# First layer's last modulation round moved out of the mixing into the output projection: products and sums on VectorE

## The chip, the core and the metric

The kernel runs on one core of one Trainium2 chip. The metric is the device time of one execution in microseconds (us), as the median of several runs. The engines are named as in the profile: PE (TensorE matmuls; PEld is its weight load), DVE (VectorE), ACT (ScalarE), POOL (GpSimd) and SP (SyncE, which here only issues DMAs). Each engine runs its own queue in order.

## The reference

The program is a diffusion backbone with two trunk layers, 512 latent tokens and 256 context tokens of width 1024, in fp32. Cut to what matters here, one layer is:

```python
def modulation(cvec, w_mod, b_mod):
    m = (jax.nn.silu(cvec) @ w_mod + b_mod)[..., None, :]
    return jnp.split(m, 6, axis=-1)

def trunk_layer(...):
    sh1, sc1, ga1, sh2, sc2, ga2 = modulation(c, w_mod, b_mod)
    sh1c, sc1c, ga1c, sh2c, sc2c, ga2c = modulation(c_ctx[None], w_mod, b_mod)
    u = (rmsnorm(x, g_mix) * (1 + sc1) + sh1) @ w_in
    ...
    mix = jnp.concatenate([pool_mixer(...), gla_output(...), latent_attention(...)], axis=-1) @ w_out
    x = x + ga1 * mix
    x = x + ga2 * squared_relu_mlp(rmsnorm(x, g_mlp) * (1 + sc2) + sh2, w_up, w_down)
    # in the first layer the context tokens get the same with their own six vectors
```

`w_mod` is 1024 x 6144 for each layer. Its six groups of 1024 columns give shift, scale and gate of the mixing (sh1, sc1, ga1) and of the MLP (sh2, sc2, ga2), for two streams: the latent tokens (from c) and the context tokens (from c_ctx). The MLP's scale sc2 is needed at the first norm before the MLP, and its gate ga2 only when the MLP's first results are added to X.

## The kernel before

All large products are fp32 split into a high and a low part, in three passes: hi x hi, hi x lo and lo x hi. A weight tile arrives by DMA as `raw` (three buffers), ACT makes its high part `whi` (L159) and DVE the low part `wlo` (L78). High and low parts live in two rings of buffers, tags "hi" and "lo", five each.

The modulation of a layer is made in three rounds of 2048 columns. Round 0 is (sh1, sc1), round 1 is (ga1, sh2), round 2 is (sc2, ga2). In the first layer rounds 1 and 2 are the function `modulation_round`. For each of eight k-steps it loads two 512 KB tiles `rawm` straight into buffers of the "hi" and "lo" rings, and PE multiplies them by the two streams' vectors, `sstat`, in four column groups of a PSUM tile `pm` (L190). `mod_end` then adds the bias row `brow` on DVE (L199), transposes on PE (L202), copies to `modT` on DVE (L203), and for gates writes rows to a DRAM tensor `gaD` with DMAs issued by POOL (L209). `load_ga` reads a gate back, spread over 128 partitions, with a DMA issued by ACT.

These rounds run inside the mixing stage, as a generator that is advanced one step at a time. A string for each layer, `STEPS`, gives the order: g is a step of the gated linear attention (GLA), a of the projections, m of the modulation and t of the softmax attention. In the first layer, `STEPS` has sixteen m, eight for each of the two rounds. The second layer's modulation is made elsewhere, during the first layer's MLP: `modulation_sums` forms the products and sums on DVE (L229, the first on ACT, L227), and PE only adds the 128 partitions of the sum up with a selecting matrix `osel` (L238).

After the mixing come, in order:

- the output projection. The first 512 columns of `w_out` are made for six token tiles, 24 matmuls each, in the PSUM tiles `op` (three buffers). The second 512 columns are made in three pairs of tiles (two buffers of a pair each). For each tile `out_res` multiplies by the gate into `rtmp` on DVE (L1162) and adds to the residual `X` (L1163; POOL for the first half of the columns, DVE for the second). A pair whose columns are complete is normalized by `norm_pair`: squares and sums on ACT (L275), the reciprocal root `rstd` on POOL, `xn` on DVE (L285), transposes `ptr` on PE (L292), then scale and shift by `scT` and `shT` into `h2h` (ACT, L300) and `h2l` (L305).
- the first up block of the MLP (`fm_pair`, L330), interleaved with the last pairs' transposes, and then the other blocks of up and down.

A scheduler puts the instructions of each engine in order when the program is built, from the order of the code and the buffers; on the chip that order is fixed.

Of the kernel before, what the change touches and what calls it, by code (L numbers as in the profile page):

```python
# [10 lines left out]
F32 = mybir.dt.float32  # L11
F32R = mybir.dt.float32r
I32 = mybir.dt.int32
AF = mybir.ActivationFunctionType
ALU = mybir.AluOpType
# [6 lines left out]
KT = 8  # L22
# [2 lines left out]
LEVELS = (1, 2, 4, 8, 16, 32, 64)  # L25
C_GV, C_GG, C_R, C_AQ = 768, 1024, 1280, 1312
GT = 5
STEPS = ("agamagamgaamgaagmaagmagamagamagamagagamagamagamagamgaamgaagmaagmagamagamttgtgttg"
         "tgttgtttgttgttttgttttgtt",
         "aaggggagaggaaagaaggaaaaaagaaaagaaaggaagaaggatatgatttttgaatgt"  # L30
         "tgtttgggtttgttggttttgtttgt")
# [3 lines left out]
def hybrid_kernel(ctx, tc, x, c, cx, c_ctx, w_mod, b_mod, g_mix, w_in, w_pool, s_pool, w_gate, b_gate,  # L35
                  g_gla, g_q, g_k, w_out, g_mlp, w_up, w_down, g_final, k_mask, k_rope, k_edge, k_invw, out):
    nc = tc.nc
    V, A, G, T = nc.vector, nc.scalar, nc.gpsimd, nc.tensor
# [3 lines left out]
    wp = ctx.enter_context(tc.tile_pool(name="wp", bufs=5))  # L42
# [9 lines left out]
    def nm(s):  # L52
        uid[0] += 1
        return f"{s}_{uid[0]}"

    def slot(s, dt=F32, w=NT):
        return sp.tile([128, w], dt, tag="S", name=nm(s))

    def wide(s, dt=F32):

        return sp.tile([128, 2 * NT + 32], dt, tag="W", name=nm(s), bufs=2)
# [12 lines left out]
    def psC(s):  # L74
        return pc.tile([128, 512], F32, tag="pc", name=nm(s))
# [11 lines left out]
    ident = const.tile([128, 128], F32, name="ident")  # L87
    make_identity(nc, ident)

    osel = const.tile([128, 2, 32], F32, name="osel")  # L90
# [21 lines left out]
    sstat = const.tile([128, KT, 32], F32, name="sstat")  # L112
# [31 lines left out]
    def wload(*srcs, sl=False):  # L144

        shp = [128, srcs[0].shape[1], sum(s_.shape[2] for s_ in srcs)]
        n = shp[1] * shp[2]
        raw = wp.tile([128, n], F32, tag="raw", name=nm("raw"), bufs=3)
        rv = raw.rearrange("p (a b) -> p a b", b=shp[2])
        o = 0  # L150
        for s_ in srcs:
            nc.sync.dma_start(rv[:, :, o:o + s_.shape[2]], s_)
            o += s_.shape[2]
        if sl:
            hi, lo = slot("whi", F32R, w=n), slot("wlo", F32R, w=n)
        else:
            hi = wp.tile([128, n], F32R, tag="hi", name=nm("whi"))
            lo = wp.tile([128, n], F32R, tag="lo", name=nm("wlo"))
        A.activation(hi, raw, AF.Copy)  # L159
        sub_lo(lo, raw, hi)  # L160
        return hi.rearrange("p (a b) -> p a b", b=shp[2]), lo.rearrange("p (a b) -> p a b", b=shp[2])

    def wcols(w, c0, n, ksplit, *more, sl=False):

        parts = []
        step = KT // ksplit
        for s in range(ksplit):
            parts.append(wload(*(w[s * step * 128:(s + 1) * step * 128, a:a + m].rearrange("(k p) n -> p k n", p=128)
                                 for a, m in ((c0, n),) + more), sl=sl))
        return lambda k: (parts[k // step][0][:, k % step], parts[k // step][1][:, k % step])  # L170
# [7 lines left out]
    gaD = dp.tile([2, 2, 2, D], F32, name="gaD")  # L178
    xD = dp.tile([NL, D], F32, name="xD")

    def modulation_round(l, r, modT):
        pm = psC("pm")
        for k in range(KT):
            yield
            for h in range(2):
                raw = wp.tile([128, 1024], F32, tag="lo" if h else "hi", name=nm("rawm"))
                c0 = r * 2048 + h * 1024
                nc.sync.dma_start(raw, w_mod[l, k * 128:(k + 1) * 128, c0:c0 + 1024])
                for j in (2 * h, 2 * h + 1):
                    T.matmul(pm[32 * j:32 * j + 32, :], sstat[:, k, :], raw[:, (j % 2) * 512:(j % 2) * 512 + 512],  # L190
                             start=(k == 0), stop=(k == KT - 1), skip_group_check=True)
        mod_end(l, r, modT, pm)
# [18 lines left out]
    def modulation_sums(l, r, modT, streams):  # L211
# [27 lines left out]
                             start=(s == 0), stop=(s == streams - 1), skip_group_check=True)  # L239
        mod_end(l, r, modT, pm)  # L240

    def mod_vec(modT, idx, s):

        r, j0 = idx // 2, (idx % 2) * 2
        return modT[:, r, j0:j0 + 2, :, s]

    def load_ga(l, which, s):
        t = bp.tile([128, D], F32, tag="ga", name=nm("ga"), bufs=2)
        nc.scalar.dma_start(t, gaD[l, which, s].partition_broadcast(128))
        return t  # L250
# [56 lines left out]
    def new_hT(s):  # L307
        return [(slot(s + "h", F32R), slot(s + "l", F32R)) for _ in range(KT)]
# [79 lines left out]
    def fin_scale(l, M, which):  # L388
        modT, scT, shT = M
        o = l * NV + 8 * which  # L390
        g_ = vec[:, o:o + 8].rearrange("p (j c) -> p j c", j=2)
        for s in range(2):
            V.scalar_tensor_tensor(scT[:, which, s].rearrange("p (j c) -> p j c", j=2), mod_vec(modT, 3 * which + 1, s),
                                   1.0, g_, ALU.add, ALU.mult)
            V.tensor_copy(shT[:, which, s].rearrange("p (j c) -> p j c", j=2), mod_vec(modT, 3 * which, s))

    def run(g):
        for _ in g:
            pass
# [9 lines left out]

    def mod_rest(l, M):  # L410
        yield from modulation_round(l, 1, M[0])
        yield from modulation_round(l, 2, M[0])
        fin_scale(l, M, 1)

    def mod_all(l, M):
        yield from modulation_sums(l, 0, M[0], 2)
# [6 lines left out]
    MODS = [None, None]  # L423
    for l in range(2):
        both = l == 0
# [6 lines left out]
        modT, scT, shT = MODS[l]  # L432
        hT = hT1 if l else new_hT("hT")
        if l == 0:
# [4 lines left out]
            rawm = {}  # L439
# [695 lines left out]
        ths = {"g": gla_thread(), "a": at_, "m": mods, "t": att_}  # L1135
        for ch in STEPS[l]:
            if ch == "t":
# [13 lines left out]
        for p2 in range(len(live) // 2):  # L1151
            XP[p2] = bp.tile([128, 2, D], F32, tag=f"X{p2}", name=nm("X"))
            t0 = 2 * p2 * 128
            src = xD[t0:t0 + 256] if l else (x[0, t0:t0 + 256] if p2 < 2 else cx[0])
            nc.scalar.dma_start(XP[p2], src.rearrange("(t p) d -> p t d", p=128))
            X[2 * p2], X[2 * p2 + 1] = XP[p2][:, 0], XP[p2][:, 1]
        ga = [load_ga(l, 0, s) for s in range(2 if both else 1)]
        def out_res(t, cb, ps):

            sl = slice(cb * 512, (cb + 1) * 512)  # L1160
            tmp = bp.tile([128, 512], F32, tag="rtmp", name=nm("rtmp"), bufs=2)
            V.tensor_tensor(tmp, ps, ga[0 if t < 4 else 1][:, sl], ALU.mult)  # L1162
            (V if cb else G).tensor_tensor(X[t][:, sl], X[t][:, sl], tmp, ALU.add)  # L1163

        np_ = len(live) // 2
        wk = wcols(w_out[l], 0, 512, 4)
        for t in live:
            ps = psB("op")
            tm_matmul(ps, t, wk, mixT, KT)
            out_res(t, 0, ps)  # L1170
        h2 = new_hT("h2")
        msc, msh = [scT[:, 1, s] for s in range(2)], [shT[:, 1, s] for s in range(2)]
        wk = wcols(w_out[l], 512, 512, 4)
        for p2 in range(np_):
            ps = psA("op")
            for i in range(2):
                tm_matmul(ps[:, i * 512:(i + 1) * 512], 2 * p2 + i, wk, mixT, KT)
                if p2 and i == 0:
                    norm_pair(p2 - 1, X, h2, msc, msh, psB)
                out_res(2 * p2 + i, 1, ps[:, i * 512:(i + 1) * 512])  # L1180


        ga = [load_ga(l, 1, s) for s in range(2 if both else 1)]
        NB = HID // 512
        pend = None

# [32 lines left out]
        for b in range(NB):  # L1219
            act = []  # L1220
            for i in range(4):
                nj = 2 if both else 4
                if b == 0 and i < nj:
                    if i == 0:
                        wks = [wcols(w_up[l], j * 128, 128, 1) for j in range(nj)]
                        pss = [psA("up") for j in range(2)]
                        if nj > 2:
                            pss = [p_[:, h * 512:h * 512 + 512] for p_ in pss for h in range(2)]
                        for p2 in range(np_):
                            if p2 == np_ - 1:  # L1230
                                norm_pair(p2, X, h2, msc, msh, psB)
                            for j in range(nj):
                                fm_pair(pss[j], wks[j], h2, KT, p2)
                    ps = pss[i]
                else:
                    wk = wcols(w_up[l], b * 512 + i * 128, 128, 1)
                    ps = psA("up")
                    fm_matmul(ps, wk, h2, KT, True, both)
                r_ = slot("relu")
                A.activation(r_[:, 0:N_], ps[:, 0:N_], AF.Relu)  # L1240
                if b % 2 and i < 2:
                    w_ = wide("a", F32R)
                    ah, al = w_[:, 0:NT], w_[:, NT:2 * NT]
                else:
                    ah, al = slot("ah", F32R), slot("al", F32R)
                V.tensor_tensor(r_[:, 0:N_], r_[:, 0:N_], r_[:, 0:N_], ALU.mult)
                A.activation(ah[:, 0:N_], r_[:, 0:N_], AF.Copy)
                sub_lo(al[:, 0:N_], r_[:, 0:N_], ah[:, 0:N_])
                act.append((ah, al))
                next(mods, None)  # L1250
            if pend is not None:
                down(*pend)
            pend = (act, b)
# [88 lines left out]
```

## Time and profile before

| what | value |
|---|---|
| median of 3 runs | 1676.79 us (1674.35 to 1676.84) |
| profiled execution: its own time | 1671.28 us |
| profiled execution: span | 1669.1 us |
| mean granted clock of TensorE | 0.985 |
| first matmul of the first layer's output projection | 363.86 us after the span's start |
| last wait in the first up block, before the matmuls of its third and fourth tile | until 460.5 us |

A row of the page's groups or of the timeline names line, engine, operation, output tile <- input tiles, and durations; "[x <-DVE rtmp]" says how long the engine was idle before and which instruction released it. The rows of the window view give, after the stretch and its length, the busy time and number of instructions of PE, PEld, DVE, ACT and POOL, then the granted clock, the DMA share and GB/s. Durations come from the one profiled execution, whose time is 0.3% below the median of the three runs.

### The profile page before, as it was taken

What the parts mean: (1) busy time and instruction counts of PE and PEld (TensorE: products, weight loads), DVE (VectorE), ACT (ScalarE), POOL (GpSimd) and SP (SyncE); (2) the same over time, 40 slices, a digit from 0 to 9 for tenths busy, and PEclk for the clock granted to TensorE, in tenths of its full rate; (3) what the DMA queues carried; (4) which work ended last, traced back from release to release, by engine and by line L of the source; (5) the groups of instructions that cost most, each with busy time, mean ns of one, the idle gap of its engine ahead of it and who ended that gap; (6) DMA issues with size and microseconds to landing.
All of it is one profiled execution on the core that took longest, in us unless ns stands there. A gap on an engine that the chain in (4) does not pass through costs nothing.

```text
span 1669.1 us, 27434 instructions
## 1 busy us (share of the span) xinstructions
PE 1595.7 (96%) x11403; PEld 1306.2 (78%) x11403; DVE 923.3 (55%) x1330; ACT 630.9 (38%) x1074; POOL 406.4 (24%) x476
## 2 busy tenths in 40 slices
PE   7999979999999999999999999897999999999997
PEld 4888856678888888888888789785667888888886
DVE  5437666753673654636546563587763545455554
ACT  5545445561531312213113234555662523223332
POOL 1121311212303041130321462241201122222224
PEclk9999989999999999999999999998999999999999
DMA  9445400222340422515424332100032313333331
GB/s 330 128 135 175 149 2 7 98 93 59 102 139 26 141 97 59 176 50 172 150 65 170 103 108 81 40 2 2 33 121 75 111 54 101 101 101 101 101 101 51
DMA packets 136636, 163.31 MB, mean 98 GB/s; under 512 B 9908, under 2 KB 108608, under 8 KB 136512
## 3 DMA queue, kind: packets, MB, share of 16 engines
q1 hardware_dynamic: 130176, 148.41, 27.9%
q10 hardware_dynamic: 5824, 13.12, 2.1%
q8 instruction: 89, 1.46, 0.4%
q14 instruction: 35, 0.29, 0.1%
q0 software_dynamic: 512, 0.03, 0.0%
HBM read 157.31 MB, written 4.23 MB: 97 GB/s over the span
## 4 chain that ended last, share of the span: by engine, by line
PE 84%; DVE 6%; ACT 4%; DMA 2%; issue 2%; POOL 2%; SPq 0%; ACTq 0%; DVEq 0%; POOLq 0%
PE dn L340 25%; PE up L321 19%; PE tm L340 7%; PE op L340 6%; PE up L323 5%; PE fm L321 4%; PE av L1071 3%; PE pT L1054 2%; PE up L330 2%; PE fm L323 1%; PE sc L1033 1%; PE att L769 1%; PE sc L1034 1%; DVE nmx L1036 1%; PE pm L190 1%
## 5 line engine op out<-in xcount | busy, mean ns | idle before, releaser
L159 ACT ACTIVATE whi<-raw 128x1024 fp32r<-128x1024 f32 (+2 forms) x182 | 185.3, 1033 | 568.0 <-PE dn L340 293.0
L1194 POOL TENSOR_TENSOR X<-X,rtmp 128x512 f32<-128x512 f32 x158 | 216.1, 1370 | 640.4 <-DVE rtmp L1193 640.1
L78 DVE TENSOR_TENSOR wlo<-raw,whi 128x1024 fp32r<-128x1024 f32 (+2 forms) x182 | 223.6, 1237 | 213.4 <-ACT whi L159 211.7
L1193 DVE TENSOR_TENSOR rtmp<-dn,ga 128x512 f32<-128x512 f32 x160 | 109.5, 689 | 212.8 <-PE dn L340 211.3
L340 PE MATMUL dn<-whi,ah 128*128 128x512 f32 x480 | 187.3, 390 | 0.6 <-ACT whi L159 0.6
L340 PE MATMUL dn<-whi,al 128*128 128x512 f32 x480 | 187.2, 390 | 0.0
L340 PE MATMUL dn<-wlo,ah 128*128 128x512 f32 x480 | 186.2, 390 | 0.0
L321 PE MATMUL up<-h2h,whi 128*128 128x512 f32 x464 | 182.5, 393 | 1.5 <-ACT relu L1240 1.5
L321 PE MATMUL up<-h2h,wlo 128*128 128x512 f32 x464 | 182.9, 394 | 0.0
L321 PE MATMUL up<-h2l,whi 128*128 128x512 f32 x464 | 182.4, 393 | 0.0
L340 PEld LDWEIGHTS dn<-whi,ah 128*128 128x128 f32 x480 | 90.1, 188 | 22.0 <-ACT whi L159 1.0
L321 PEld LDWEIGHTS up<-h2h,whi 128*128 128x128 f32 x464 | 87.1, 188 | 24.1 <-ACT relu L1240 1.7
L340 PEld LDWEIGHTS dn<-wlo,ah 128*128 128x128 f32 x480 | 90.1, 188 | 19.5 <-DVE wlo L78 0.5
L340 PEld LDWEIGHTS dn<-whi,al 128*128 128x128 f32 x480 | 90.1, 188 | 19.4
L340 PE MATMUL tm<-whi,hTh 128*128 128x256 f32 (+1 forms) x352 | 102.3, 292 | 1.1 <-ACT UV L891 1.1
L321 PEld LDWEIGHTS up<-h2h,wlo 128*128 128x128 f32 x464 | 87.1, 188 | 19.6
L321 PEld LDWEIGHTS up<-h2l,whi 128*128 128x128 f32 x464 | 87.1, 188 | 19.3
L340 PE MATMUL tm<-whi,hTl 128*128 128x256 f32 (+1 forms) x352 | 100.7, 287 | 0.0
L340 PE MATMUL dn<-whi,a 128*128 128x512 f32 x320 | 100.0, 395 | 0.4 <-DVE rtmp L1193 0.4
L340 PE MATMUL tm<-wlo,hTh 128*128 128x256 f32 (+1 forms) x352 | 100.2, 288 | 0.0
L229 DVE SCALAR_TENSOR_TENSOR macc<-rawm,sstat,macc 128x1024 f32<-128x1024 f32 x56 | 76.3, 1383 | 8.2 <-DMA rawm<-in_w_mod_dram 7.7
L1036 DVE TENSOR_REDUCE nmx<-sc 128x1 f32<-128x768 f32 x64 | 60.5, 955 | 24.1 <-PE sc L1034 23.3
(293 smaller groups left out, 3320.6 us busy)
## 6 DMA issues: line engine op xcount, KB each, us to landing
rawm<-in_w_mod_dram SPq DMA_DIRECT2D x80, 512.0 KB, 5.2
raw<-in_w_up_dram SPq DMA_DIRECT2D x64, 512.0 KB, 4.5
raw<-in_w_down_dram SPq DMA_DIRECT2D x64, 512.0 KB, 4.6
raw<-in_w_in_dram SPq DMA_DIRECT2D x26, 512.0 KB, 3.9
rawm<-in_w_mod_dram SPq DMA_DIRECT2D x32, 256.0 KB, 5.3
raw<-in_w_out_dram SPq DMA_DIRECT2D x16, 512.0 KB, 4.7
raw<-in_w_in_dram SPq DMA_DIRECT2D x12, 256.0 KB, 2.8
ga<-gaD ACTq DMA_DIRECT2D x6, 512.0 KB
```

The lines of the kernel that those rows point to most:

```text
L78: V.tensor_tensor(lo, full, hi.bitcast(F32), ALU.subtract)
L159: A.activation(hi, raw, AF.Copy)
L229: V.scalar_tensor_tensor(acc[s], raw, c_, acc[s], ALU.mult, ALU.add)
L321: T.matmul(ps[:, 0:NL], a, b[:, 0:NL], start=st, stop=sp_)
L323: T.matmul(ps[:, NL:NT], a, b[:, NL:NT], start=st, stop=sp_)
L330: T.matmul(ps[:, cs], a, b[:, cs], start=(k == 0 and i == 0), stop=(k == nk - 1 and i == 2))
L340: T.matmul(ps, a[:, sl], bb, start=(k == 0 and i == 0), stop=(k == nk - 1 and i == 2))
L1036: V.tensor_reduce(nmx[:, i:i + 1], sv, AX.X, ALU.max, negate=True)
L1054: T.transpose(pt_[:, i * 128:(i + 1) * 128], p_[:, ki * 128:(ki + 1) * 128], ident)
L1071: T.matmul(av_[64 * hh:64 * hh + 64, 0:256], vst, pe[:, hh * 256:hh * 256 + 256], start=(ki == 1), stop=(ki == len(kts) - 2))
L1193: V.tensor_tensor(tmp, ps, ga[0 if t < 4 else 1][:, sl], ALU.mult)
L1194: (V if b == NB - 1 and not both and t == 3 else G).tensor_tensor(X[t][:, sl], X[t][:, sl], tmp, ALU.add)
```

## The change

Round 2 of the first layer leaves the mixing. Eight of the sixteen m of `STEPS` are removed. A new generator `modulation_half` makes 1024 columns of a round: for each of eight k-steps one 512 KB load, and for each of the two streams a multiply-add into an accumulator `acc` (named macc) on DVE; for k = 0 two scaled copies on ACT. At the end eight matmuls of 256 columns with `osel` add up the partitions, then follow bias, two transposes and copies to `modT`. The first half is sc2, then comes `fin_scale`, which makes scT and shT; the second half is ga2, which ends with eight DMAs to `gaD` from POOL. The generator `mod_late` is advanced one step before the first projection tile and two steps after each tile; what is left runs before the MLP. The two gate loads of the first layer's MLP move behind the up matmuls of block 1, ahead of the first down block. The second layer is as before.

```diff
-STEPS = ("agamagamgaamgaagmaagmagamagamagamagagamagamagagamagamgaamgaagmaagmagamagamttgtgttg"
+STEPS = ("agamagagaamgaagaagmagaagamagaagagamagaagamagagaamgaagaagmaagagamagaagamttgtgttg"
...
+    def modulation_half(l, r, h, modT):
+        acc = [wide("macc")[:, 0:1024] for _ in range(2)]
+        c0 = r * 2048 + h * 1024
+        for k in range(KT):
+            yield
+            raw = wp.tile([128, 1024], F32, tag="lo" if k % 2 else "hi", name=nm("rawm"))
+            nc.sync.dma_start(raw, w_mod[l, k * 128:(k + 1) * 128, c0:c0 + 1024])
+            for s in range(2):
+                c_ = sstat[:, k, s:s + 1]
+                if k == 0:
+                    A.activation(acc[s], raw, AF.Copy, scale=c_)
+                else:
+                    V.scalar_tensor_tensor(acc[s], raw, c_, acc[s], ALU.mult, ALU.add)
+        yield
+        brow = wp.tile([128, 1024], F32, tag="raw", name=nm("brow"), bufs=3)[:, 0:256]
+        pm = psC("pm")
+        for j in range(4):
+            nc.sync.dma_start(brow[32 * j:32 * j + 32], b_mod[l, c0 + j * 256:c0 + j * 256 + 256].partition_broadcast(32))
+            for s in range(2):
+                T.matmul(pm[32 * j:32 * j + 32, 0:256], osel[:, s], acc[s][:, j * 256:j * 256 + 256],
+                         start=(s == 0), stop=(s == 1), skip_group_check=True)
+        V.tensor_tensor(brow, pm[:, 0:256], brow, ALU.add)
+        pt = psC("pt")
+        for cc in range(2):
+            T.transpose(pt[:, cc * 128:(cc + 1) * 128], brow[:, cc * 128:(cc + 1) * 128], ident)
...
+        if (r, h) != (2, 0):
+            for s in range(2):
+                for j in range(4):
+                    nc.gpsimd.dma_start(gaD[l, r - 1, s:s + 1, j * 256:(j + 1) * 256], brow[32 * j + s:32 * j + s + 1, :])
...
     def mod_rest(l, M):
         yield from modulation_round(l, 1, M[0])
-        yield from modulation_round(l, 2, M[0])
+
+    def mod_late(l, M):
+        yield from modulation_half(l, 2, 0, M[0])
         fin_scale(l, M, 1)
+        yield from modulation_half(l, 2, 1, M[0])
...
+        late = mod_late(l, MODS[l]) if both else iter(())
+        def late_steps(n):
+            for _ in range(n):
+                next(late, None)
         wk = wcols(w_out[l], 0, 512, 4)
+        late_steps(1)
         for t in live:
             ps = psB("op")
             tm_matmul(ps, t, wk, mixT, KT)
             out_res(t, 0, ps)
+            late_steps(2)
...
                 out_res(2 * p2 + i, 1, ps[:, i * 512:(i + 1) * 512])
-        ga = [load_ga(l, 1, s) for s in range(2 if both else 1)]
+                late_steps(2)
+        run(late)
+        if not both:
+            ga = [load_ga(l, 1, s) for s in range(1)]
...
+            if b == 1 and both:
+                ga = [load_ga(l, 1, s) for s in range(2)]
             if pend is not None:
                 down(*pend)
```

The order of the instructions shows three places. The first is DVE in the output projection, in the second 512 columns. Before the change its queue holds there the multiplies by the gate (rtmp), the additions to X and the norm (xn) of the first pair of tiles; op_4622 is that pair and op_4677 the next:

```order
L1162 TENSOR_TENSOR rtmp_4579<-op_4554,ga_4388 128x512
L78 TENSOR_TENSOR wlo_4921<-raw_4918,whi_4920 128x1024
L1162 TENSOR_TENSOR rtmp_4647<-op_4622,ga_4386 128x512
L1163 TENSOR_TENSOR X_4380<-X_4380,rtmp_4647 128x512
L285 TENSOR_SCALAR xn_4702<-X_4380,rstd_4705 128x1024
L1162 TENSOR_TENSOR rtmp_4674<-op_4622,ga_4386 128x512
L1162 TENSOR_TENSOR rtmp_4764<-op_4677,ga_4386 128x512
L1163 TENSOR_TENSOR X_4380<-X_4380,rtmp_4674 128x512
```

After the change the same pair is op_4609, and the lines of the old code are some 35 higher (L1199 is L1162 of before, L1200 is L1163, L319 is L285):

```order
L427 SCALAR_TENSOR_TENSOR scT_125<-modT_124,vec 128x8 x2
L1199 TENSOR_TENSOR rtmp_4634<-op_4609,ga_4301 128x512
L255 SCALAR_TENSOR_TENSOR macc_4527<-rawm_4641,sstat,macc_4527 128x1024
L255 SCALAR_TENSOR_TENSOR macc_4528<-rawm_4641,sstat,macc_4528 128x1024
L1200 TENSOR_TENSOR X_4295<-X_4295,rtmp_4634 128x512
L255 SCALAR_TENSOR_TENSOR macc_4527<-rawm_4672,sstat,macc_4527 128x1024
L255 SCALAR_TENSOR_TENSOR macc_4528<-rawm_4672,sstat,macc_4528 128x1024
L319 TENSOR_SCALAR xn_4705<-X_4295,rstd_4708 128x1024
L255 SCALAR_TENSOR_TENSOR macc_4527<-rawm_4676,sstat,macc_4527 128x1024
L255 SCALAR_TENSOR_TENSOR macc_4528<-rawm_4676,sstat,macc_4528 128x1024
L1199 TENSOR_TENSOR rtmp_4669<-op_4609,ga_4301 128x512
L1199 TENSOR_TENSOR rtmp_4767<-op_4680,ga_4301 128x512
```

Products of the second half (k-steps 4 to 6 here; 1 to 3 stand further ahead) now stand between the multiply of the pair's first tile, its addition, its norm, and the multiply of the second tile.

The second place is SP's queue, which issues the loads. Before, the eight tiles of w_out stand behind the last modulation loads of the mixing, and the up weights behind them:

```order
L188 DMA rawm_2808<-in_w_mod_dram 128x1024
L152 DMA raw_4390<-in_w_out_dram 128x2x512
L152 DMA raw_4396<-in_w_out_dram 128x2x512
L152 DMA raw_4402<-in_w_out_dram 128x2x512
L152 DMA raw_4408<-in_w_out_dram 128x2x512
L152 DMA raw_4598<-in_w_out_dram 128x2x512
L152 DMA raw_4604<-in_w_out_dram 128x2x512
```

After the change the first four w_out tiles are followed by the bias rows and the first loads of the first half, among them the fifth and sixth w_out tile:

```order
L152 DMA raw_4317<-in_w_out_dram 128x2x512
L152 DMA raw_4323<-in_w_out_dram 128x2x512
L260 DMA brow_4503<-in_b_mod_dram 32x256 x4
L249 DMA rawm_4359<-in_w_mod_dram 128x1024
L152 DMA raw_4585<-in_w_out_dram 128x2x512
L249 DMA rawm_4363<-in_w_mod_dram 128x1024
L152 DMA raw_4591<-in_w_out_dram 128x2x512
L249 DMA rawm_4395<-in_w_mod_dram 128x1024
L249 DMA rawm_4399<-in_w_mod_dram 128x1024
```

The seventh and eighth w_out tile stand behind three loads of the second half.

The third place is PE between the sixth tile of the first 512 columns (op_4554 before, op_4533 after) and the first pair of the second. Before, the one follows the other directly:

```order
L340 MATMUL op_4554<-whi_4410,mixh_3907 128x512
L340 MATMUL op_4554<-whi_4410,mixl_3908 128x512
L340 MATMUL op_4554<-wlo_4411,mixh_3907 128x512
L340 MATMUL op_4622<-whi_4600,mixh_3457 128x512
L340 MATMUL op_4622<-whi_4600,mixl_3458 128x512
```

After, the eight matmuls that add up the first half's accumulators stand in between (two streams, macc_4329 and macc_4330, by turns):

```order
L374 MATMUL op_4533<-wlo_4326,mixh_3822 128x512
L262 MATMUL pm_4504<-macc_4329,osel 32x256
L262 MATMUL pm_4504<-macc_4330,osel 32x256
L262 MATMUL pm_4504<-macc_4329,osel 32x256
L262 MATMUL pm_4504<-macc_4330,osel 32x256
...
L374 MATMUL op_4609<-whi_4587,mixh_3372 128x512
L374 MATMUL op_4609<-whi_4587,mixl_3373 128x512
L374 MATMUL op_4680<-whi_4587,mixh_3372 128x512
```

PE thus cannot begin the second 512 columns before the first half's last products are done.

More of the change, by code (lines that the diff above doesn't have):

```diff
@@ L27 @@
 GT = 5
-STEPS = ("agamagamgaamgaagmaagmagamagamagamagagamagamagamagamgaamgaagmaagmagamagamttgtgttg"
+STEPS = ("agamagagaamgaagaagmagaagamagaagagamagaagamagagaamgaagaagmagaagamttgtgttg"
          "tgttgtttgttgttttgttttgtt",
@@ L240, in modulation_sums @@
         mod_end(l, r, modT, pm)
+    def modulation_half(l, r, h, modT):
[23 more added lines that the diff above has]
+            T.transpose(pt[:, cc * 128:(cc + 1) * 128], brow[:, cc * 128:(cc + 1) * 128], ident)
+        src = pt[:, 0:256].rearrange("p (c j r) -> p j c r", c=2, j=4)
+        for a in range(2):
+            V.tensor_copy(modT[:, r, 2 * h + a].rearrange("p (b c) s -> p b c s", b=2), src[:, 2 * a:2 * a + 2, :, 0:2])
+        if (r, h) != (2, 0):
+            for s in range(2):
+                for j in range(4):
+                    nc.gpsimd.dma_start(gaD[l, r - 1, s:s + 1, j * 256:(j + 1) * 256], brow[32 * j + s:32 * j + s + 1, :])
     def mod_vec(modT, idx, s):
```

## The prediction

> **What bounds the kernel now.** I first read the busy times and the chain of waits on the page.
>
> ```profile
> span 1669.1 us, 27434 instructions
> PE 1595.7 (96%) x11403; PEld 1306.2 (78%) x11403; DVE 923.3 (55%) x1330; ACT 630.9 (38%) x1074; POOL 406.4 (24%) x476
> PE 84%; DVE 6%; ACT 4%; DMA 2%; issue 2%; POOL 2%; SPq 0%; ACTq 0%; DVEq 0%; POOLq 0%
> ```
>
> PE is busy for 96% of the span and is 84% of the chain that ended last, so work taken off PE can shorten the run, and work that makes PE wait lengthens it. The mean says little about one place, so I next cut out the stretches that the change touches: the second modulation round in mixing (160 to 222 us), the attention behind it (222 to 262), the output projection (363.9 to 434) and the first up block (434 to 460).
>
> ```profile
> 160.00:180.00 20.00, 19.91 (x225) 15.31 (x226) 14.33 (x33) 10.59 (x19) 5.47 (x10) 1.00 0.90 304
> 180.00:200.00 20.00, 19.92 (x306) 15.85 (x304) 12.14 (x22) 8.63 (x16) 9.14 (x18) 1.00 0.19 57
> 200.00:222.00 22.00, 22.00 (x291) 17.43 (x290) 12.06 (x28) 7.42 (x11) 4.87 (x6) 1.00 0.13 46
> 222.00:245.00 23.00, 13.99 (x427) 10.92 (x425) 18.54 (x34) 13.04 (x27) 5.53 (x13) 0.78 0.01 3
> 363.90:398.40 34.50, 34.50 (x154) 27.64 (x155) 12.73 (x16) 8.33 (x10) 9.11 (x7) 1.00 0.30 95
> 398.40:434.00 35.60, 35.14 (x166) 29.03 (x165) 15.43 (x24) 10.53 (x17) 6.23 (x11) 1.00 0.28 81
> 434.00:460.00 26.00, 22.24 (x172) 20.40 (x170) 19.89 (x35) 17.90 (x33) 11.29 (x14) 1.00 0.43 130
> ```
>
> After the stretch come the busy us of PE, PEld, DVE, ACT and POOL, then the granted clock, the DMA share and GB/s. From 160 to 222 PE has no gap, and VectorE (DVE) is about 60% busy. The output projection is the same: PE busy 69.64 of 70.10 us, DVE 28.16. So both the place the work leaves and the place it goes to are full on PE and have room on DVE. Whether that room can be used depends on the order in DVE's queue.
>
> **What is removed: eight modulation steps on PE.**
>
> ```profile
> L190 PE MATMUL pm<-rawm,sstat x128: 592/592/617, 81.1 to 220.8; 128*32 128x512 f32 x128
> 192.30 1.07 PE L190 MATMUL pm<-rawm,sstat 128*32 128x512 f32 x8
> 193.30 1.02 PE L769 MATMUL att<-gq,KK 64*32 64x32 f32 x96
> 223.45 0.66 PE L202 MATMUL pt<-ident,brow 128*128 128x128 f32 x4
> ```
>
> The 128 records are two rounds of eight k-steps with 8 records each. One step holds PE from 192.30 to the next matmul at 193.30, 1.00 us. Eight steps are 8.0 us, and the round's four transposes take 0.6 more (0.66, overlapping the next): **-8.6 us**. All eight steps lie in stretches where PE never waits, so I take the full value. The upper end is 10.0: the round's last operations on DVE stand in 222 to 245, where DVE has 18.54 of 23 us and PE waits for it.
>
> ```profile
> 221.90 0.68 DVE L199 TENSOR_TENSOR brow<-pm,brow 128x512 f32<-128x512 f32 x1
> 225.08 0.19 DVE L203 COPY modT<-pt 128x32 f32<-128x32 f32 x1
> 225.30 0.53 DVE L393 SCALAR_TENSOR_TENSOR scT<-modT,vec 128x8 f32<-128x8 f32 x2
> ```
>
> These are 0.68 + 0.19 + 0.53 = 1.4 us. The lower end is 4: if the GLA and attention chains, which must still run through ACT and DVE, become late as soon as PE arrives earlier, half of the removal is lost. The sixteen loads (512 KB each) go with it; they were hidden.
>
> **What is added on PE.** Each half has eight 32x256 matmuls and two transposes. The nearest row is the layer-1 version with 512 columns.
>
> ```profile
> 552.73 1.91 PE L238 MATMUL pm<-macc,osel 128*32 128x512 f32 x8
> 554.57 0.50 PE L321 MATMUL up<-h2h,whi 128*128 128x512 f32 x1
> ```
>
> Four matmuls (8 records) take 1.84 us there, in the order a, b, a, b of two column groups. In the removed round four matmuls in four groups took 1.00. I read this as a pair in different groups overlapping: 0.92 per pair of 512 columns, so about 0.47 for one matmul of 256 columns. The new order is a, a, b, b, c, c, d, d. If only neighbours of different groups overlap, that is five times 0.47 = 2.35 us; if none do, eight times 0.47 = 3.8. I take 2.35, plus 0.35 for two transposes (half of 0.66): 2.7 per half, 5.4 in all. The Trainium skill (TensorEngine Tiling (Array Packing), Key Properties) says that different tiles of the array can run matmuls in parallel; the 1.00 us against 1.84 agrees. By that rule the sum has 2.35, and 3.8 without any overlap.
>
> **When the first half is ready.** The order of the instructions is known; what I work out is when each starts.
>
> ```profile
> 358.20 15.34 SPq L152 DMA_DIRECT2D raw<-in_w_out_dram  x8
> ...
> rawm<-in_w_mod_dram SPq DMA_DIRECT2D x80, 512.0 KB, 5.2
> ...
> raw<-in_w_in_dram SPq DMA_DIRECT2D x26, 512.0 KB, 3.9
> ...
> raw<-in_w_out_dram SPq DMA_DIRECT2D x16, 512.0 KB, 4.7
> ...
> 464.14 2.48 DVE L229 SCALAR_TENSOR_TENSOR macc<-rawm,sstat,macc 128x1024 f32<-128x1024 f32 x2
> 452.00 1.15 ACT L227 ACTIVATE macc<-rawm,sstat 128x1024 f32<-128x1024 f32 x1
> ```
>
> The eight w_out issues run from 358.2 to 373.5; the first new load stands behind four of them and four bias loads, about 368.3 (an estimate). With 4.7 us to land it is there at 373.0. Loads rotate through five "hi" and five "lo" buffers, but w_out holds four of each until the sixth tile, so one hi and one lo buffer turn over. A buffer's round is landing 4.7 plus the pair of products, 2.48: 7.2. On the hi side: 373.0, plus 2.2 for two ACT copies, plus three rounds of 7.2 = 396.8 for k6. The k7 products follow (2.5), and output rows of the tiles in between cost about 0.9: **400.2**.
>
> ```profile
> 387.47 0.69 DVE L1162 TENSOR_TENSOR rtmp<-op,ga 128x512 f32<-128x512 f32 x1 [4.75 <-PE op L340]
> 392.91 0.69 DVE L1162 TENSOR_TENSOR rtmp<-op,ga 128x512 f32<-128x512 f32 x1 [4.75 <-PE op L340]
> 395.12 3.95 DVE L78 TENSOR_TENSOR wlo<-raw,whi 128x1024 fp32r<-128x1024 f32 x3 [1.52 <-ACT whi L159]
> 404.47 0.69 DVE L1162 TENSOR_TENSOR rtmp<-op,ga 128x512 f32<-128x512 f32 x1 [1.57 <-PE op L340]
> 415.35 0.50 PE L340 MATMUL op<-whi,mixh 128*128 128x512 f32 x1 [0.46 <-DVE rtmp L1162]
> ```
>
> Tile five of six ends at 392.91 and one tile is 5.44 us (387.47 to 392.91, 24 matmuls of 0.227), so PE reaches the new matmuls at 398.35. It waits 1.9 us there, works 2.35, and the half-width bias addition (half of 0.68, say 0.4) ends at 403.0.
>
> **When the second half lets the projection go on.** In before, PE starts the third pair of tiles at 415.35, right behind the multiply of the first pair's second tile (ended 415.31). In the new queue of DVE the same multiply stands behind twelve products of the second half. From 403.0 DVE has, in order up to it: six pairs of products, 6 x 2.48 = 14.9; two wlo at 1.23, 2.5; modT and scT, 0.9; one multiply, one addition to X and one xn, with the rows below, 2.2; then the multiply itself, 0.7. That is 21.2.
>
> ```profile
> L78 DVE TENSOR_TENSOR wlo<-raw,whi 128x1024 fp32r<-128x1024 f32 x13 | 15.9, 1223 | 9.2 <-ACT whi L159 8.8
> L1163 DVE TENSOR_TENSOR X<-X,rtmp 128x512 f32<-128x512 f32 x6 | 4.1, 714 | 0.0
> L285 DVE TENSOR_SCALAR xn<-X,rstd 128x1024 f32<-128x1024 f32 x6 | 4.5, 752 | 6.3 <-POOL rstd L258 6.3
> ```
>
> DVE also waits inside the list: the load of step k6 can start only when k4's products end, and until its turn DVE has one pair and xn, 3.2 us, against 4.7 for landing, so 1.5; k5 by the same sum 0.3. Together 424.2 + 1.8 = 426.0 against 415.3: **10.7 us late**, the first half's PE work included. PE's own list could have been there at 419.3 (398.35 + 1.9 + 2.35 + 0.35 + 72 matmuls, 16.3), so it stands some 6.7 us in pieces of 1 to 3.3 us. The second half's 2.7 us of PE come on top: **+13.4**.
>
> **Other edits.** The gate loads move behind the first up block and wait for eight small writes from POOL instead of four; I value this and POOL's eight issues at 0. Their cover is the first up block; if it is gone, h2l on POOL is late by the issues.
>
> ```profile
> gaD<-brow POOLq DMA_DIRECT2D x16, 2.0 KB, 3.3
> ```
>
> The bounds are +3 (one landing of 3.3 shows) and -2 (of the 3.8 us that PE waits in 434 to 460, half disappears because ACT and POOL get ahead). The sum is -8.6 + 13.4 = **+4.8 us**. The profiled execution took 1671.28 us (span 1669.1), 0.3% below the median 1676.79 of the three runs shown; added to that median this gives **1681.5**. The late part's bounds are 9.6 (landing 3.9 as w_in's: k7 is ready when PE comes, saving 1.9, and the waits on DVE vanish, 1.8) and 18.7 (landing 5.2, five rounds of 0.5, and 3.8 per matmul group, 2.9).
>
> **Rivals.** (1) The queues keep up and only PE's 5.4 remains: -8.6 + 5.4 = -3.2, 1673.6. For it speaks that DVE has 28 of 70 us busy and the products add about 35; against it, DVE takes its rows in order, and the twelve products stand ahead of what PE waits for. (2) The clock falls. The chip shows this already:
>
> ```profile
> 226.00:230.00 4.00, 1.18 (x3) 0.49 (x3) 3.81 (x8) 2.09 (x5) 0.59 (x1) 0.74 0.00 0
> 230.00:234.00 4.00, 2.51 (x99) 1.99 (x99) 3.64 (x8) 1.81 (x5) 0.93 (x4) 0.50 0.01 4
> PE qT L1097 <- DVE qs L78: 2.3, 1, 2.3
> ```
>
> With single waits up to 2.3 us around 226 the granted clock is 0.50 a little later, while 434 to 460, with 3.8 us of waits in small pieces, stays at 1.00. Two windows of 4 us at half clock cost 4 us: 1685.5. It decides where PE is busy under about half of 4 us; the pieces here leave it around 75% busy, so I hold it less likely. The Trainium skill (TensorE: Matmul & The Clock Gate, Why this matters for your kernels) wants no PE gap over about 3 us, or the clock goes to half; the trace shows half clock after shorter gaps in a sparse stretch, and by the rule only the longest gap, 3.3 us, would trigger it. (3) Mixing does not give the 8.6 but 4, since its DVE and ACT chains are late next: -4 + 13.4, 1686.2.
>
> **How the numbers follow.** Forecast 0.52, rival one 0.20, clock 0.15, mixing 0.13. The range, **1672.5 to 1688.5**, reaches from rival one to beyond rivals two and three. The bounds of all terms together would be wider but need every one at its end. A measurement of this kernel can tell about 0.2%, 3.35 us, from no change. Rival one lies on that border: half of it, and a little of the forecast, is faster, 0.14; within, the other half and the forecast's lower part, 0.30; slower 0.56.
>
> **What would show it.** In the new profile: no pm matmuls of the second round between 160 and 222, and the attention behind earlier by about 8.6 us; PE waiting for macc before the first new matmuls (about 2 us), and for rtmp before the third pair (about 3); waits of DVE for rawm; the new matmul groups at 2.35 us; the clock at 1.00 there. The forecast is wrong if the stretch from the first projection matmul to the end of the first up block grows by under 9 us, or mixing shortens by under 7.

## The result and the profile after

The changed kernel takes 1686.26 us (median of 4, 1683.86 to 1690.17) against 1675.57 us before (median of 4): ratio 1.0073, 95% interval 1.0059 to 1.0087, that is 12 us by the ratio. The forecast was +4.8 us. The sign held, and the range too, near its upper end of 1688.5; the size was less than half of what came. All ratios here compare fast executions; one execution of e2, at 3138.04 us, was slow and stands outside its ratio.

The two `STEPS` strings printed under "The change" differ by some letters from those of the kernels. In the kernels the first layer's string has 17 m before and 9 after, because the last m ends the generator. The modulation steps are sixteen and eight, as told.

The page of the changed kernel, busy times and chain, stands against the first lines of the prediction:

```profile
span 1688.3 us, 27428 instructions
PE 1602.8 (95%) x11371; PEld 1312.6 (78%) x11371; DVE 962.2 (57%) x1362; ACT 635.6 (38%) x1078; POOL 412.3 (24%) x480
PE 82%; DVE 6%; ACT 4%; DMA 4%; issue 2%; POOL 2%; ACTq 0%; SPq 0%; DVEq 0%; POOLq 0%
```

PE lost two points of the chain, and DMA rose from 2% to 4%. PE's busy time rose by 7 us, in part because the same matmuls take longer where the clock is lower (0.43 us instead of 0.23 around 424 us). The first projection matmul shows what arrived from mixing. The PE timeline of before, and then of the changed kernel:

```profile
363.79 0.50 PE L340 MATMUL op<-whi,mixh 128*128 128x512 f32 x1
```

```profile
359.46 0.50 PE L374 MATMUL op<-whi,mixh 128*128 128x512 f32 x1
```

It comes 4.3 us earlier, not 8.6. From there to the last wait of the first up block (for relu, at 460.5 before and 475.3 after) it is 96.7 us before and 115.9 after: 19.2 more, not 13.4. The windows of the changed kernel (columns as in the prediction) show gaps and a lower clock in both places:

```profile
180.00:200.00 20.00, 18.25 (x326) 15.89 (x323) 12.23 (x25) 5.32 (x12) 6.36 (x12) 0.83 0.01 2
...
398.40:450.00 51.60, 43.92 (x208) 33.73 (x207) 39.47 (x52) 15.39 (x24) 13.77 (x22) 0.93 0.50 150
450.00:480.00 30.00, 24.70 (x161) 21.84 (x161) 24.31 (x35) 19.25 (x33) 9.35 (x13) 0.89 0.43 134
```

In before, 180 to 222 had 0.1 us of gaps and a clock of 1.00, and so had the whole stretch from 363.9 to 460 apart from some 4 us of gaps. To split a stretch I use windows of 2 us at even times (those at its ends count by their share, which moves the entries by up to 0.4 us): idle is the window less PE's busy time, clock loss is busy time times (1 - granted clock), and the rest is work at full clock.

| from the first projection matmul to the up block's last wait | length | idle | clock loss | work |
|---|---|---|---|---|
| before | 96.7 | 4.3 | 0.0 | 92.4 |
| changed | 115.9 | 13.7 | 4.1 | 98.2 |
| changed, second profile (e12) | 115.8 | 13.6 | 4.4 | 97.9 |

The two profiles of the changed kernel agree within 0.3 us, so the excess does not belong to one execution alone. It is 9.4 us of waiting, 4.1 us of clock and 5.8 us of work.

### The profile page after: what moved, and what is told of

Same layout as the page of the kernel before. It is cut to its first block, busy times and chain, and to the rows that moved or that the text cites. A ratio compares the mean times of both kernels' runs of the same rounds, so it can differ in the third digit from the quotient of the medians.

```text
span 1688.3 us, 27428 instructions
## 1 busy us (share of the span) xinstructions
PE 1602.8 (95%) x11371; PEld 1312.6 (78%) x11371; DVE 962.2 (57%) x1362; ACT 635.6 (38%) x1078; POOL 412.3 (24%) x480
## 4 chain that ended last, share of the span: by engine, by line
PE 82%; DVE 6%; ACT 4%; DMA 4%; issue 2%; POOL 2%; ACTq 0%; SPq 0%; DVEq 0%; POOLq 0%
PE dn L374 24%; PE up L355 19%; PE tm L374 7%; PE op L374 5%; PE up L357 5%; PE fm L355 4%; PE av L1108 3%; PE pT L1091 3%; PE up L364 2%; PE fm L357 1%; DMA rawm<-in_w_mod_dram 1%; PE sc L1070 1%; DMA raw<-in_w_out_dram 1%; PE sc L1071 1%; PE att L806 1%
```

## The experiments

Each is a variant of the changed kernel, timed in five rounds beside the kernel before. Ratios are to before. e1 and e3 to e6 leave part of the computation out; the others make all of it.

**Taking the parts apart.** e1 leaves the second round out; e2 leaves mixing as before and makes the round again, late.

```diff
     def mod_rest(l, M):
         yield from modulation_round(l, 1, M[0])
+        fin_scale(l, M, 1)              # e1; round 2 copied from round 1
...
-        late = mod_late(l, MODS[l]) if both else iter(())
+        late = iter(())                 # e1
+        yield from modulation_round(l, 2, M[0])   # e2, with the old string
```

> The second round of the first layer is left out altogether (the MLP's scale and gate take the first round's values), so mixing has eight modulation steps as in the changed kernel and nothing comes later. Theory one (the forecast's term): all 8.6 us of TensorE time come back, 1667 us, ratio 0.995. Theory two (in the new profile the first projection matmul comes only 4.3 us earlier, since TensorE then waits for the GLA chain near 192 us and the granted clock falls behind it): about 1671 us, ratio 0.9974. If the clock loss was chance of that one execution, theory one's number or little above.

> Mixing is that of the kernel before, with all sixteen steps; the second round is made again, late, as in the changed kernel, and overwrites the first result. Only the late part is added. Theory one (forecast): +13.4 us over before, 1689 us, ratio 1.008. Theory two (the new profile: 19.3 us from the first projection matmul to the end of the first up block, 5.5 of it clock): +15 to +19, 1691 to 1695, ratio 1.009 to 1.0115. If the two parts simply add, e1's change plus this one's gives the changed kernel's +10.7.

e1: 0.9966 (0.9953 to 0.9980), -5.7 us. e2: 1.0115 (1.0094 to 1.0135), +19.2 us. Their sum, 13.5, is the changed kernel's +12 within the intervals. So the parts add, mixing gives back two thirds of its 8.6, and the late part costs nearly half again as much as the forecast 13.4, more also than the 18.7 given as its upper bound. e1's mixing has the same three waits as the changed kernel. PE's waits from 60 to 225 us in the changed kernel (total, times, longest), where before has one, of 1.3 (left out is one in the attention at the window's end, where before waits too):

```profile
...
PE att L806 <- issue: 1.7, 1, 1.7
PE tm L374 <- ACT UV L928: 1.2, 1, 1.2
PE pm L190 <- DMA rawm<-in_w_mod_dram: 0.9, 2, 0.7
```

The first of these stands at 191.7, just where before had two modulation steps (192.30 and 194.25) around the same GLA matmuls. The profile does not name what ended it ("issue"); that it is the GLA chain is read from its place. Behind it the clock falls; the windows of the changed kernel and then of its second profile:

```profile
192.00:196.00 4.00, 2.60 (x31) 2.24 (x32) 3.34 (x10) 0.00 (x0) 0.00 (x0) 0.54 0.02 4
196.00:200.00 4.00, 4.00 (x33) 3.34 (x32) 0.72 (x2) 0.98 (x2) 0.00 (x0) 0.61 0.00 0
```

```profile
196.00:200.00 4.00, 4.00 (x50) 3.40 (x31) 2.04 (x5) 0.15 (x1) 0.00 (x0) 0.68 0.02 4
```

**Can another choice of steps cover that wait?** e6 is e1 with the later steps of the old string kept, instead of every second one.

```diff
-STEPS = ("agamagagaamgaagaagmagaagamagaagagamagaagamagagaamgaagaagmagaagamttgtgttg"
...
+STEPS = ("agaagagaagaagaagagaagaagaagagamagamagamagamgaamgaagmaagmagamagamttgtgttg...
```

> As e1 (second round left out, nothing late), but the modulation steps that stay in mixing are the later ones of the old string, not every second one. Theory one (the old steps near 192 us covered a wait for the GLA chain, so their removal opened the gap and dropped the clock): that gap is filled again, and 3 to 4 us come on top of e1, ratio 0.994 to 0.995. Theory two (the chain's waits only move to another place): ratio as e1's, 0.9966.

e6: 0.9999 (0.9991 to 1.0008), worse than e1 and than both theories. With one modulation step back beside it, the wait near 192 falls to 1.2 us and the clock stays at 1.00 there, as theory one had it. But PE now waits 3.3 us for QQ of the GLA chain, from 119.2 to 122.4 with half clock behind it, and 2.2 us for modulation loads. So theory two comes nearer: the modulation steps were filling; taking them out leaves waits, wherever they fall.

**What makes the late part long?** e3 drops 12 of its 16 loads, e4 14 of its 28 products, e5 both.

```diff
+            if k < 2:                                    # e3, e5
                 raw = wp.tile([128, 1024], F32, tag="lo" if k % 2 else "hi", name=nm("rawm"))
                 nc.sync.dma_start(raw, w_mod[l, k * 128:(k + 1) * 128, c0:c0 + 1024])
...
-                else:
+                elif s == 0:                             # e4, e5
                     V.scalar_tensor_tensor(acc[s], raw, c_, acc[s], ALU.mult, ALU.add)
```

> The late part loads only the tiles of k-steps 0 and 1 of each half and uses the second for steps 1 to 7, so 12 of 16 loads are left out; the products on VectorE are all there, in nearly the same order. Theory one (VectorE's queue is what makes TensorE late): only the waits for loads go, 2 us, 1684. Theory two (the turn-over of the buffers and the loads, with w_out's seventh tile issued at 397 us, sets the pace): 6 to 9 us go, 1677 to 1680.

> The late part makes the products of one stream only (the other keeps its step 0), so 14 of 28 products of 1.28 us leave VectorE's queue and all loads stay. Theory one (VectorE's queue): the rows ahead of the multiply that TensorE waits for shrink by 6 x 1.28 = 7.7 us, 1677 to 1679. Theory two (buffers and loads): the rounds of a buffer shrink from 7.2 to 5.9 us, so about 4 us go, 1682.

> Both cuts at once: two loads per half and products of one stream only (12 of 16 loads and 14 of 28 products left out). Each cut alone gave nothing (ratios 1.0064 and 1.0077 against 1.0073 of the changed kernel). Theory one (two chains of nearly equal length, products on VectorE and loads through two buffers, each late enough alone): together 7 to 10 us go, ratio 1.001 to 1.003. Theory two (neither matters; the time is lost to the sums' place among TensorE's matmuls, the order of the third pair and the clock): still 1.006 to 1.008.

e3: 1.0064 (1.0047 to 1.0082); e4: 1.0077 (1.0057 to 1.0098); e5: 1.0001 (0.9985 to 1.0017). Neither cut alone can be told from the changed kernel; both together take off 12 us. In the same stretch as in the table e3 has 114.7 us, e4 113.5 and e5 102.7. The timeline of DVE in e4 shows why half of the products do not help:

```profile
403.22 1.23 DVE L78 TENSOR_TENSOR wlo<-raw,whi 128x1024 fp32r<-128x1024 f32 x1 [0.44 <-ACT whi L159]
408.51 2.60 DVE L255 SCALAR_TENSOR_TENSOR macc<-rawm,sstat,macc 128x1024 f32<-128x1024 f32 x2 [4.06 <-DMA rawm<-in_w_mod_dram]
411.03 0.69 DVE L1199 TENSOR_TENSOR rtmp<-op,ga 128x512 f32<-128x512 f32 x1
```

DVE has become idle, but the multiply at 411.03 stands behind a product that waits 4.06 us for its load. With all products and few loads (e3) the same place is filled with products. The late part has two limits of nearly equal length, and a single queue that makes PE's multiply wait for the longer. In the changed kernel the chain of waits goes through both by turns (start, duration, what; steps of under 0.1 us between the lines are left out):

```profile
394.32 1.27 DVE macc L255
...
396.12 1.22 DVE wlo L78
397.35 5.72 DMA raw<-in_w_out_dram
403.16 1.06 ACT whi L159
404.27 1.07 DVE wlo L78
405.40 1.28 DVE macc L255
406.70 5.28 DMA rawm<-in_w_mod_dram
412.09 2.48 DVE macc L255 x2
414.57 0.61 DVE X L1200
...
418.96 2.47 DVE macc L255 x2
421.44 0.61 DVE rtmp L1199
422.09 8.87 PE op L374 x26
```

The load of w_out at 397.35 is one that the forecast counted no wait for: its buffer came free only when DVE, behind the first half's products, had made the wlo of an earlier tile. The last line is 26 matmuls in 8.87 us, 0.341 each on average instead of 0.227: the clock.

```profile
416.00:420.00 4.00, 1.44 (x7) 0.71 (x6) 3.27 (x4) 0.42 (x2) 1.67 (x2) 1.00 0.65 204
420.00:424.00 4.00, 1.91 (x5) 1.52 (x6) 4.00 (x6) 1.06 (x1) 0.00 (x0) 0.62 0.11 43
424.00:428.00 4.00, 4.00 (x11) 3.13 (x10) 3.36 (x4) 1.15 (x2) 0.96 (x2) 0.52 0.00 2
```

PE is busy for 3.35 of the 8 us from 416 to 424; half clock sets in within them, and lasts to 428.

**Products on PE.** e8 keeps the place and lets PE make the products.

```diff
-                    V.scalar_tensor_tensor(acc[s], raw, c_, acc[s], ALU.mult, ALU.add)
+            for j in range(4):
+                T.matmul(pm[32 * j:32 * j + 32, 0:256], sstat[:, k, :], raw[:, j * 256:j * 256 + 256],
+                         start=(k == 0), stop=(k == KT - 1), skip_group_check=True)
```

> The late round stays where the change has it, but TensorE makes the products itself, as in mixing (four 256-column matmuls per step), and VectorE has none. Added on TensorE: 16 steps of about 0.5 us, 8, and transposes 0.7. Theory one (VectorE's queue): only those 8.7 and some waits for loads, against -4.7 from mixing: ratio 1.002 to 1.004. Theory two (loads through the two buffers, now waited for by TensorE itself): as the changed kernel or worse, 1.007 to 1.010.

e8: 1.0068 (1.0055 to 1.0081). The ratio is near theory two's, but not by its reason: the stretch has 113.5 us, of it 7.6 idle, 1.7 clock loss and 104.2 work. The waits of the changed kernel are mostly gone (PE waits 2.1 us for a load), and the added work, 11.8 us where I had 8.7, takes their place. Equal times here have different contents. It also narrows what e4 showed: where DVE has no products, the same loads hold PE for only 2.1 us, so in this profile the loads are not a limit by themselves but by the turns that they take with DVE's products.

**Moving the products out of the way.** e7 spreads the first half over the projection with its bias rows in a buffer of their own, and puts the second half into the MLP's first block. e9 puts the second half behind the last norms of the first up block. e11 is e9 with the first half exactly as the change has it. In e9 to e11 the second half's accumulators also lie in other buffers (tag "xn"), and the second layer's modulation starts five up tiles later.

```diff
-            late_steps(2)                 # after each tile of the first 512 columns
+            late_steps(1)                 # e7, e9
-        brow = wp.tile([128, 1024], F32, tag="raw", name=nm("brow"), bufs=3)[:, 0:256]
+        brow = lay.tile([128, 512], F32, tag="brow", name=nm("brow"))[:, 0:256]   # e7, e9
...
-        acc = [wide("macc")[:, 0:1024] for _ in range(2)]
+        acc = [wide("macc")[:, 0:1024] if h == 0 else bp.tile([128, 1024], F32, tag="xn", name=nm("macc"), bufs=2) for _ in range(2)]   # e9, e10, e11
...
+                if b == 0:
+                    late_steps(2)         # e7: second half
...
+                if 4 * b + i >= 7 or not both:
+                    for _ in range(2 if i == 0 else 1):
+                        next(mods, None)
+                elif 4 * b + i >= 2:
+                    late_steps(2)         # e9, e11: second half
```

> All of the computation, but the first half of the late round is spread one step per tile over the output projection, the second half goes into the MLP's first block, and the bias rows have a buffer of their own, outside the three of the weight loads. Theory one (what TensorE waits for is what stands ahead in VectorE's queue and in the buffers): the third pair waits for no products of the second half, the late cost falls from 17 to about 6 to 9 us, ratio about 1.000 to 1.003. Theory two (late cost from whatever is added there): as the changed kernel, 1.007.

> All of the computation. The first half of the late round is spread as in e7; the second half comes only after the last norms of the first up block, in the MLP's blocks 0 and 1, where VectorE is busy for about half of the time, and the second layer's modulation starts five up tiles later. Theory one (a product costs only where a row that TensorE waits for soon stands behind it): the up block's 13 us of loss in e7 go; left are about 3 for the first half, 1.75 for the second half's matmuls and transposes, against -5.5 from mixing: ratio 0.999 to 1.001. Theory two (the late work costs wherever it is put): 1.005 or more.

> All of the computation. The first half is exactly where the change has it (the same rows on VectorE up to the sixth tile, the same three buffers for bias and weights); only the second half is put behind the first up block, as in e9. Theory one (the second half's products ahead of the third pair's multiply are the larger part of the late loss): the first half's own part, by the changed kernel's profile 5 to 7 us up to the second 512 columns, remains, with 1.75 for the second half, against -5.5 from mixing: ratio 1.000 to 1.002. Theory two (the first half's place is what costs most): 1.004 or more.

e7: 1.0081 (1.0064 to 1.0098), a miss: the projection is nearly clean (its last tile ends 73.7 us after its first matmul, 70.7 before, 86.8 in the changed kernel), but the scheduler drew the second half's products between the norms of the up block, and there PE waits for what stands behind them. The clock falls there too, which costs 5.5 us by the table's measure. PE's waits in e7 from 432 to 476 us:

```profile
PE up L364 <- DVE h2l L339: 3.7, 2, 1.9
PE ptr L326 <- DVE full L338: 3.0, 2, 1.9
PE up L364 <- POOL h2l L339: 2.6, 1, 2.6
PE ptr L326 <- DVE xn L319: 1.8, 1, 1.8
...
```

e9, where they stand behind the norms (the same view, same window):

```profile
...
PE up L366 <- DVE h2l L341: 1.3, 2, 0.9
PE ptr L328 <- DVE xn L321: 0.7, 1, 0.7
PE up L366 <- POOL h2l L341: 0.5, 1, 0.5
```

e9: 0.9993 (0.9981 to 1.0005). The same 28 products at the same price of 1.28 us each cost 13 us less than in the changed kernel; its stretch, which now holds the first half alone, is 97.9 us long and has no clock loss. e11: 1.0021 (1.0007 to 1.0035). So of the changed kernel's loss against e9, some 9 us (1.0076 to 1.0021) belong to the second half's place (with the other buffers and the later start that go with it), and 5 us (1.0021 to 0.9993) to the first half's pace and the shared bias buffer together, which these runs do not tell apart.

**A smaller move, and the change again.** e10 keeps the MLP's scale in mixing in half-width PE steps at the old places and moves only the gate, as in e9. e12 is the changed kernel.

> All of the computation. The MLP's scale stays in mixing on TensorE (half-width steps of about 0.5 us in the old places), and only the gate's half leaves, into the MLP's blocks 0 and 1 as in e9; the projection is that of the kernel before. Theory one: -4.3 us of TensorE work in mixing, of which half to two thirds arrive, +1.75 later: ratio 0.998 to 1.000. If mixing gives nothing with half steps: 1.001.

> The changed kernel once more, for a second profile of it and a ratio from the same chip. If the losses of the first profile belong to the kernel, then again: first projection matmul about 4 to 5 us earlier than before, 17 to 19 us more to the end of the first up block with 3 to 4 us of it clock, a wait near 192 us in mixing with half clock behind it; ratio 1.006 to 1.008. If the clock's part was chance, it is absent or elsewhere.

e10: 0.9989 (0.9980 to 0.9999), the best complete version, and still within the 0.2% that this kernel's measurement can tell from no change. In it the first projection matmul comes at 355.93, 7.9 us earlier than before, although only half of the work has left. But four matmuls of the projection later PE waits for f, a tile of the attention that ACT makes:

```profile
360.78 0.50 PE L402 MATMUL op<-whi,mixh 128*128 128x512 f32 x1 [2.43 <-ACT f L1147]
```

So the early start is in part only another order; by the up block's last wait (456.5) it is 4.0 us ahead of before. The half steps still stand where PE had them as filling, there is no wait near 192 and the clock stays at 1.00 from 188 to 200; that this is the reason is argued from one profile, not shown. e12: 1.0076 (1.0064 to 1.0089), as theory one said, except that the projection began 6.0 us early (357.79). The attention ahead of it has by itself a clock loss that differs between executions: from 222 to 356 us it is 9.6 us before, 8.3 in the changed kernel and 5.2 here. A single profile's start of the projection is therefore good to a few us only.

## Why the forecast was right in sign and too small

- **-8.6 from mixing: this term failed, and its lower end, 4, was the better number.** The work left, but e1 as a whole gained 5.7, and over ten profiles with the new mixing the first projection matmul comes at 355.8 to 362.8, on average 359.3, 4.5 early. The forecast had named "mixing shortens by under 7" as a sign that it is wrong, and this sign came. My reason was "All eight steps lie in stretches where PE never waits". That PE had no gap there was because the steps filled it (the wait at 191.7, and e6). Rival three had this term nearly right and its reason too, with the wait read as the GLA chain's. That its 1686.2 us is the measured time is luck: its late part was 13.4 us, not 19.2, and the median of before that it was added to was 1.2 us higher than the one measured beside the change.
- **PE work of the late part, 5.4: right in sum (5.8), wrong in its parts, so the sum is luck.** Eight matmuls of 256 columns take 1.03 us in one go, not 2.35, as PE's timeline in e4 shows:

```profile
390.86 1.09 PE L262 MATMUL pm<-macc,osel 128*32 128x256 f32 x16 [0.27 <-DVE macc L255]
391.89 0.50 PE L374 MATMUL op<-whi,mixl 128*128 128x512 f32 x1
```

  In the changed kernel they run in two pieces for each half and take 1.6 us, 3.2 in all; the transposes take 0.3. About 2 us more stand in the projection's own matmuls: some twenty of them, most right beside a wait or a matmul of another kind, take 0.31 to 0.48 us instead of 0.23 without a lower clock; before has 8 such.
- **The first half's end, 400.2: right.** It was done at 395.6, 36.1 us behind the projection's start, where the forecast had 36.4. PE's wait there was 0.75 (0.24 and 0.51), not 1.9, because the tiles ahead ended a little later and the first of the new matmuls ran before the last product was made.
- **DVE's queue, 10.7 late: right in mechanism, a little small.** From the projection's start the multiply ended at 62.6 (422.05), against 51.5 before, 11.1 later. Part of it came through a late tile of w_out, for which the forecast had no wait and which held PE 1.6 us (2.2 in e12). The forecast read the queue as one list; e3, e4 and e5 show two limits, products and loads, each long enough.
- **Other edits, 0: not tested singly.** From the last projection tile's end to the up block's last wait the changed kernel needs 29.1 us (86.8 to 115.9 behind the projection's start), before 26.0 (70.7 to 96.7). About 1 us of the difference is clock (0.52 in 472 to 476), 1 more waiting. Whether the eight gate writes on POOL have a share in these 3 us stays open.
- **The clock, 0 in the forecast, 4 in rival two: it is 4.1 to 4.4 us in the late part and 1.6 to 3.2 in mixing (125 to 222 us, ten profiles; before none).** It was not an alternative to the forecast but came with it. I had held it less likely because PE would be 75% busy over the whole stretch; what stands ahead of the fall is a few us with little work, 3.35 of 8. The half clock of the up block's end also lasts beyond the stretch, to 480, which costs 1.5 us more than the table has.

So -8.6 + 13.4 became about -5 + 19 by the profiles, and -5.7 + 19.2 by e1 and e2. The measured 12 lies a little below their sum, within the intervals.

## What to carry to other kernels

An instruction on an engine with room still costs if something that the bottleneck waits for soon stands behind it in that engine's queue: find the row that the full engine waits for, and put background work behind it, not in front (e7 and e9 differ in this, in the accumulators' buffers and in a later start of the second layer's modulation, and by 0.9%). Work that fills the gaps of a dependent chain is worth less than its duration when it is taken away; here two thirds (e1) or nothing (e6). And before cutting one cost of a late chain, see whether a second of equal length runs beside it: e3 and e4 each gained nothing, e5 gained 12 us.

## What was unexpected of the hardware

- One wait of 1.75 us on PE (191.65 to 193.40), in a stretch that is otherwise full, was followed by a granted clock of 0.54 and 0.61 in the windows from 192 to 200. The Trainium skill (TensorE: Matmul & The Clock Gate, Why this matters for your kernels) names gaps over about 3 us as the danger; here one gap well under that, 1.66 to 2.19 us, was followed by half clock in each of the ten profiles with the new mixing. In e6 the wait at the same matmuls was 1.16 us, and the clock stayed at 1.00.
- Eight small matmuls in the order of groups a, a, b, b, c, c, d, d took 1.03 us, 0.13 each. The row that the forecast had gone by gives 0.46 for one of 512 columns, so 0.23 at the same overlap. The removed step has as many columns in each of its four groups and takes 1.00, so the four groups seem to overlap even in this order.
